# One inversion for all chunks of a delta-rule recurrence, with split masks and units every third step

## The chip, the cores and the metric

The kernel runs on one core of one Trainium2 chip. The metric is the device time of one execution in microseconds (us). Before the change the median of three runs is 2544.13 us (2540.35 to 2546.16).

## What is computed

A two-layer decoder trunk on 272 tokens (16 learned ones and 256 of the input) of width 2048 in float32. Layer 0 mixes tokens with RWKV-7, layer 1 with gated linear attention; an MLP with squared ReLU follows each. The change touches layer 0 alone, whose core in the reference is a step by step recurrence over a 64x64 state for each of 32 heads:

```python
def step(S, inp):
    r_t, w_t, k_t, v_t, a_t, b_t = inp
    sa = jnp.einsum('bhvk,bhk->bhv', S, a_t)
    S = S * w_t[:, :, None, :] + sa[..., None] * b_t[:, :, None, :] + v_t[..., None] * k_t[:, :, None, :]
    y = jnp.einsum('bhvk,bhk->bhv', S, r_t)
    return S, y
```

## The kernel before

The kernel does not step token by token. It cuts the 272 tokens into four chunks of 64 and a short one of 16 (padded to 32). For each chunk and head it forms a score matrix of 128x128 (`AM0` to `AM3`, all 32 heads of a chunk in one tile; `AMr`, 64x64, for the short chunk) whose left half holds what a triangular system needs and whose right half what the output needs. The triangular part of 64x64 is inverted: its two 32x32 diagonal blocks by elimination on VectorE (`eliminate`, 30 steps of two operations), then joined on TensorE (`merge`, a first and a second product with four copies behind each).

Two stages matter here. In the first, the projection of v, TensorE makes 256 steps of three matrix products (`mm3`; a weight tile in two float32r parts, `hi` cast by ScalarE at L132, `lo` subtracted by VectorE at L133, lasts 8 steps). Between the steps the code places score "units": one unit loads four pairs of heads of one chunk (two DMAs into a `ring` of three slots), makes 32 products of scores into two PSUM banks (`scores`, L500; the banks come from the tags `pu` and `pt`, two banks each), and four steps later VectorE multiplies them by a mask into `AM`. There are 16 units of full chunks and 4 of the short one. The chunks 0 and 1 are inverted in this stage (`invert(0)`, from step 49) and merged in it; the chunks 2 and 3 (`invert(1)`) are begun at step 245 and run into the second stage.

The second stage is the recurrence: five chunks, two groups z of 16 heads each, in an order written out by hand. `centre` and `keys` transpose values and keys into place, `inner` and `state` form the right-hand side (two halves of a bank are negated by `sides`, the first by ScalarE, the second by VectorE), `solve` multiplies by the inverse, `learn` updates the state `S`, `emit` makes the output and `gate` the output gate. The merges of chunks 2 and 3 stand in the rounds c = 1 and c = 2 of it.

The order on TensorE and VectorE is the order of the program text (`manual_schedule`). The elimination is cut into pieces, and `fill` puts the next piece into VectorE's order as soon as two clocks of a planner allow it (`pe` and `dve` advance them by costs written in the code; VectorE's may run `slack` us ahead of TensorE's; `fill(True)` empties the queue). ScalarE's and SyncE's orders are left to a scheduler that takes the earliest ready one. Two engines that read one PSUM bank are put one behind the other by semaphores.

Of the kernel before, what the change touches and what calls it, by code (L numbers as in the profile page):

```python
# [17 lines left out]
P = 128  # L18
# [10 lines left out]
C = 64  # L29
# [16 lines left out]
class Kern:  # L46
# [217 lines left out]
    def rwkv(self, done):  # L264
# [222 lines left out]
        TA, X, T2 = (self.t(kp, [P, 32, 32], n) for n in ("TA", "X", "T2"))  # L487
        X4 = T2.rearrange("p a b -> p (a b)")[0:64, :512].rearrange("p (a b) -> p a b", a=16)
        sb = self.t(kp, [P, KT, HEAD], "S")
        amof = lambda c: AMs[c] if c < NC4 else AMr  # L490

        def scores(t, c, g, bank):
# [9 lines left out]
            pe(0.95)  # L502
            return lambda: mask(c, g, pv, n)

        def mask(c, g, pv, n):
            mk = self.maskA if c < NC4 else self.maskR
            for q in range(2):
# [3 lines left out]
        upd = lambda n: self.t(kp, [P, 256], "upd", 1)[:, :n]  # L511
# [24 lines left out]
        def eliminate(X, n, rows):  # L536
            k = rows.stop - rows.start
            x = X[rows]
            for s in range(1, n - 1):
                a, m = n - 1 - s, s  # L540
                yield cost(a * m)
                w = upd(a * m)[rows].rearrange("p (a b) -> p a b", a=a)
                tt(w, x[:, s + 1 : n, s : s + 1].to_broadcast([k, a, m]), x[:, s : s + 1, :m].to_broadcast([k, a, m]))
                yield cost(a * m)
                tt(x[:, s + 1 : n, :m], x[:, s + 1 : n, :m], w, ALU.add)

        def invert(i):
            bands = [(2 * i + a, b) for a in range(2) for b in range(2)]
            diag = lambda c, u: AMs[c][64 + 32 * u : 96 + 32 * u, :, 32 * u : 32 * u + 32]
            halves = (slice(0, 16), slice(16, 32))  # L550
            for b, (c, u) in enumerate(bands):
                nc.scalar.copy(TA[32 * b : 32 * b + 32], diag(c, u))
            for k in halves:
                yield 1.15
                nc.vector.transpose(X[:, k], TA.rearrange("p h t -> p t h")[:, k])
            nc.gpsimd.memset(X.rearrange("p a b -> p (a b)")[:, ::33], 1.0)
            yield from eliminate(X, 32, slice(0, P))
            for k in halves:
# [654 lines left out]
```

## Time and profile before

| | |
|---|---|
| median of 3 runs | 2544.13 us |
| profiled execution | 2551.34 us, its span 2549.6 us |
| TensorE (PE) busy | 98% of the span |
| VectorE (DVE) busy | 64% |
| ScalarE (ACT) busy | 49% |
| granted TensorE clock, mean | 0.994 |
| projection of v | about 282 to 409.7 us |
| recurrence | 409.7 to about 503 us |

A busy TensorE is not one at its peak, since matrix products are pipelined; what tells is where it stands idle and what ended the idle time. An idle VectorE or ScalarE costs nothing by itself.

### The profile page before, as it was taken

How to read it: one execution, taken by the hardware profiler on the slowest of the kernel's cores; microseconds unless marked ns; L12 is line 12 of the kernel's file. 1: busy time of each engine (PE TensorE's matmuls, PEld its weight loads, DVE VectorE, ACT ScalarE, POOL GpSimd, SP SyncE). 2: the span in 40 equal slices, each digit the busy share in tenths (PEclk: the TensorE clock that was granted, in tenths of full speed). 3: DMA queues.
4: the chain of work that ended last, by engine and by line, in shares of the span. 5: the costliest groups of instructions: out<-in, count | busy, mean ns of one | idle time of the engine just before them, and what ended most of it. 6: DMA issues, size and time to landing. Idle time of an engine off the chain costs nothing.

```text
span 2549.6 us, 47710 instructions
## 1 busy us (share of the span) xinstructions
PE 2493.8 (98%) x19636; PEld 2328.4 (91%) x19636; DVE 1638.3 (64%) x2568; ACT 1252.6 (49%) x1990; POOL 7.2 (0%) x31
## 2 busy tenths in 40 slices
PE   7999999899999999999999999999999999999997
PEld 7998898789999999999999999998888888888886
DVE  8777787586555455455456688777666656666565
ACT  5476536464444344344344455544555445445344
POOL 0000000000000000000000000000000000000000
PEclk9999999899999999999999999999999999999999
DMA  5578865155555555555555454445555555555554
GB/s 196 185 244 276 261 213 190 40 177 174 174 174 174 173 169 177 174 173 173 174 173 180 163 168 160 154 156 174 187 187 189 190 187 187 188 190 189 186 189 157
DMA packets 156970, 461.64 MB, mean 181 GB/s; under 512 B 15312, under 2 KB 44240, under 8 KB 156752
## 3 DMA queue, kind: packets, MB, share of 16 engines
q1 hardware_dynamic: 156752, 458.59, 54.6%
q8 instruction: 154, 2.52, 0.4%
q14 instruction: 64, 0.52, 0.1%
HBM read 441.49 MB, written 17.04 MB: 180 GB/s over the span
## 4 chain that ended last, share of the span: by engine, by line
PE 87%; DVE 2%; ACT 2%; DMA 2%; issue 1%; SPq 0%; DVEq 0%; ACTq 0%
PE pj L166 24%; PE pj L138 14%; PE pj L139 14%; PE pj L140 14%; PE pj L167 13%; DMA ca<-cad 1%; DVE lo L133 1%; DMA ard<-ar 1%; PE pt L737 1%; ACT hi L132 0%; PE pu L1051 0%; PE pt L139 0%; PE pt L623 0%; PE pt L140 0%; PE pu L500 0%
## 5 line engine op out<-in xcount | busy, mean ns | idle before, releaser
L132 ACT CAST hi<-raw 128x1024 fp32r<-128x1024 f32 (+2 forms) x820 | 812.8, 997 | 1105.4 <-PE pj L139 586.9
L133 DVE TENSOR_TENSOR lo<-raw,hi 128x1024 fp32r<-128x1024 f32 (+2 forms) x820 | 946.6, 1159 | 613.9 <-ACT hi L132 606.3
L138 PE MATMUL pj<-x,hi 128*128 128x272 f32 x2144 | 624.4, 291 | 4.5 <-ACT x L305 4.5
L139 PE MATMUL pj<-x,hi 128*128 128x272 f32 x2144 | 620.8, 290 | 2.6 <-DVE x L266 2.1
L140 PE MATMUL pj<-x,lo 128*128 128x272 f32 x2144 | 619.3, 289 | 1.0 <-DVE lo L133 0.9
L166 PE MATMUL pj<-x,hi 128*128 128x512 f32 x1664 | 587.3, 396 | 2.1 <-DVE cj L176 1.1
L167 PE MATMUL pj<-x,lo 128*128 128x256 f32 x1664 | 468.5, 282 | 0.8 <-DVE lo L133 0.8
L139 PEld LDWEIGHTS pj<-x,hi 128*128 128x128 f32 x2144 | 407.4, 190 | 5.5 <-DVE x L266 4.6
L138 PEld LDWEIGHTS pj<-x,hi 128*128 128x128 f32 x2144 | 402.9, 188 | 9.2 <-ACT x L305 5.2
L140 PEld LDWEIGHTS pj<-x,lo 128*128 128x128 f32 x2144 | 404.3, 189 | 2.4 <-DVE lo L133 1.8
L166 PEld LDWEIGHTS pj<-x,hi 128*128 128x128 f32 x1664 | 312.9, 188 | 75.0 <-issue 1.9
L166 PE MATMUL pj<-h,hi 128*128 128x512 f32 x1024 | 358.5, 394 | 0.0
L167 PEld LDWEIGHTS pj<-x,lo 128*128 128x128 f32 x1664 | 314.4, 189 | 1.7 <-DVE lo L133 1.1
L138 PE MATMUL pj<-h,hi 128*128 128x272 f32 x1024 | 297.0, 290 | 0.0
L139 PE MATMUL pj<-h,hi 128*128 128x272 f32 x1024 | 295.4, 288 | 0.0
L140 PE MATMUL pj<-h,lo 128*128 128x272 f32 x1024 | 294.7, 288 | 0.0
L167 PE MATMUL pj<-h,lo 128*128 128x256 f32 x1024 | 288.5, 282 | 0.0
L166 PEld LDWEIGHTS pj<-h,hi 128*128 128x128 f32 x1024 | 192.4, 188 | 44.3
L139 PEld LDWEIGHTS pj<-h,hi 128*128 128x128 f32 x1024 | 195.1, 190 | 0.0
L140 PEld LDWEIGHTS pj<-h,lo 128*128 128x128 f32 x1024 | 193.5, 189 | 0.0
L167 PEld LDWEIGHTS pj<-h,lo 128*128 128x128 f32 x1024 | 193.5, 189 | 0.0
L138 PEld LDWEIGHTS pj<-h,hi 128*128 128x128 f32 x1024 | 192.2, 188 | 0.0
(330 smaller groups left out, 2215.7 us busy)
## 6 DMA issues: line engine op xcount, KB each, us to landing
raw<-mlp_w_d SPq DMA_DIRECT2D x512, 512.0 KB, 3.3
raw<-gla_in_d SPq DMA_DIRECT2D x98, 512.0 KB, 3.3
raw<-w_rkv_d SPq DMA_DIRECT2D x80, 512.0 KB, 3.9
raw<-gla_o_d SPq DMA_DIRECT2D x32, 512.0 KB, 3.2
raw<-rw_o_d SPq DMA_DIRECT2D x18, 512.0 KB, 3.3
raw<-w_r_d SPq DMA_DIRECT2D x16, 512.0 KB, 3.4
raw<-rw_oK_d SPq DMA_DIRECT2D x16, 448.0 KB, 3.3
ard<-ar SPq DMA_DIRECT2D x16, 320.0 KB, 4.3
```

The lines of the kernel that those rows point to most:

```text
L132: nc.scalar.copy(hi[:, h], raw[:, h])
L133: nc.vector.tensor_tensor(out=lo[:, h], in0=raw[:, h], in1=hi[:, h].bitcast(F32), op=ALU.subtract)
L138: nc.tensor.matmul(out, hi[:, ws], xh, start=first, stop=False)
L139: nc.tensor.matmul(out, hi[:, ws], xl, start=False, stop=False)
L140: nc.tensor.matmul(out, lo[:, ws], xh, start=False, stop=last)
L166: nc.tensor.matmul(wide, hi[:, ws], x[kt][:, :, off : off + SEQ], start=kt == 0, stop=False)
L167: nc.tensor.matmul(ps[:, :SEQ], lo[:, ws], x[kt][:, 0, off : off + SEQ], start=False, stop=kt == nk - 1)
L737: nc.tensor.matmul(pg, g2s[f // 4][:, f % 4, i], gs[i], start=i == 0, stop=i == 1)
```

## The change

All four chunks are inverted at once: `TA` and `X` hold two layers (the two diagonal blocks) of 128 partitions (four chunks of 32 rows), so that one elimination of 60 operations does twice the elements each. A unit comes every third step from step 4 to step 49, and the elimination starts when the last full unit is masked, at step 55. VectorE masks only the left half of each bank, ScalarE copies the right half unmasked, and `rmask` masks that half later in place, for 16 heads at a time. All eight merge products and the four short units go to the head of the recurrence and to its round c = 0. The load of the next weight tile moves from the second to the third step of a tile, and the gates of round 1 are spread over the rounds 1 and 2.

```diff
+        TA, X = (self.t(kp, [P, 2, 32, 32], n) for n in ("TA", "X"))
         sb = self.t(kp, [P, KT, HEAD], "S")
+        T2 = flat(sb).rearrange("p (a b) -> p a b", a=32)
...
             for q in range(2):
-                dve(0.73 if c < NC4 else 0.44)
-                tt(amof(c)[:, 8 * g + q : 8 * g + 8 : 2], pv[q], mk.unsqueeze(1).to_broadcast([2 * n, 4, 2 * n]))
+                am = amof(c)[:, 8 * g + q : 8 * g + 8 : 2]
+                dve(0.44)
+                tt(am[:, :, :w], pv[q][:, :, :w], mk[:, :w].unsqueeze(1).to_broadcast([2 * n, 4, w]))
+                if w < 2 * n:
+                    nc.scalar.copy(am[:, :, w:], pv[q][:, :, w:])
+
+        def rmask(z, c):
+            if c < NC4:
+                am = AMs[c][:, 16 * z : 16 * z + 16, C:]
+                dve(1.2)
+                tt(am, am, self.maskA[:, C:].unsqueeze(1).to_broadcast([P, 16, C]))
...
+        def gather(c):
+            for u in range(2):
+                at(step + 2 * u, lambda u=u: nc.scalar.copy(TA[band(c), u], diag(c, u)))
+
+        def invert():
+            by_t = lambda u: TA[:, u].rearrange("p h t -> p t h")
+            for u in range(2):
+                for k in halves:
+                    yield 1.15
+                    nc.vector.transpose(X[:, u, k], by_t(u)[:, k])
+            nc.gpsimd.memset(X.rearrange("p u a b -> p u (a b)")[:, :, ::33], 1.0)
+            yield from eliminate(X, 32, flat(sb))
             for k in halves:
                 yield 1.15
+                nc.vector.transpose(T2.rearrange("p h s -> p s h")[:, k], X[:, 0].rearrange("p t s -> p s t")[:, k])
+            for u in range(2):
+                for k in halves:
+                    yield 1.15
+                    nc.vector.transpose(by_t(u)[:, k], X[:, u, k])
+                if u == 0:
+                    nc.scalar.copy(diag(0, 0), TA[band(0), 0])
+                    nc.scalar.copy(t11(0), T2[band(0)])
+                    nc.scalar.copy(diag(1, 0), TA[band(1), 0])
+            for c in range(NC4):
+                yield 0.69
+                nc.vector.tensor_copy(diag(c, 1), TA[band(c), 1])
+                if c in (1, 3):
+                    yield 0.69
+                    nc.vector.tensor_copy(t11(c), T2[band(c)])
+                if c < 2:
+                    nc.scalar.copy(diag(c + 2, 0), TA[band(c + 2), 0])
...
-                    if j == 1 and (f, i) != (KT - 1, 1):
+                    if j == 2 and (f, i) != (KT - 1, 1):
                         ahead()
+                        dve(1.34)
...
-        def unit():
+        def unit(then):
             m = scores(*loaded.pop(0), self.pu if len(order) % 2 else self.ptr)
-            more()
-            return m
+            if order[0][0] < NC4:
+                more()
+            at(step + 4, m)
+            if then:
+                at(step + 4, then)
...
+            then = {6: lambda: gather(0), 7: lambda: gather(1), 11: lambda: gather(2),
+                    15: lambda: (gather(3), at(step + 2, lambda: todo.append([invert(), None])))}
+            for z, c, n in ((0, 0, 28), (1, 0, 31), (0, 1, 34), (1, 1, 37)):
+                at(n, lambda z=z, c=c: rmask(z, c))
+            for k in range(16):
+                at(4 + 3 * k, lambda k=k: unit(then.get(k)))
...
             slack[0] = 0.25
             inner(0, 0)
             sides(0, 0)
             bload(1, 0)
+            more()
             centre(1, 0, ("x", "x"))
             aload(0, 1)
             aload(1, 1)
+            inner(1, 0)
+            sides(1, 0)
+            keys(1, 0)
+            masks = [scores(*loaded.pop(0), self.pu)]
+            more()
+            masks.append(scores(*loaded.pop(0), self.ptr))
+            more()
+            fill(True)
+            for c in range(2):
+                merge(c, (self.pm, self.pry)[c], False, True)
+            masks[0]()
+            for c in range(2):
+                merge(c, (self.pm, self.pry)[c], True, True)
+            masks[1]()
             for c in range(5):
                 if c:
                     state(0, c)
                     learn(1, c - 1)
+                    if c > 1:
+                        rmask(0, c)
                     emit(1, c - 1)
...
                 solve(0, c)
+                if c == 0:
+                    merge(2, self.ptr, False, True)
                 if c < NC4:
                     learn(0, c)
+                    if c > 1:
+                        rmask(1, c)
                 emit(0, c)
+                if c == 0:
+                    merge(3, self.ptr, False, True)
                 solve(1, c)
...
                 if c == 0:
+                    merge(2, self.ptr, True, True)
+                    short(self.ptr)
+                    more()
                     centre(0, 2, ("x", "hi"))
+                    merge(3, self.ptr, True, True)
+                    short(self.ptr)
+                    todo.append([invert_short(), None])
```

`short` makes a unit of the short chunk and masks it at once.

## Rows read from the trace of the kernel before

**Rows 1.** The page, busy time of TensorE, its share of the span, instructions.
```profile
PE 2493.8 (98%) x19636; PEld 2328.4 (91%) x19636; DVE 1638.3 (64%) x2568; ACT 1252.6 (49%) x1990; POOL 7.2 (0%) x31
```

**Rows 2.** Stretches: from:to, length, each engine's busy us, clock, DMA share, GB/s.
```profile
290.00:300.00 10.00, 10.00 (x147) 9.03 (x147) 6.92 (x12) 2.57 (x5) 0.00 (x0) 1.00 0.94 309
...
320.00:351.00 31.00, 31.00 (x271) 30.60 (x269) 28.64 (x69) 12.86 (x25) 0.16 (x1) 1.00 0.54 181
...
392.00:409.70 17.70, 17.70 (x409) 16.49 (x398) 8.36 (x15) 16.24 (x29) 0.00 (x0) 1.00 0.49 162
409.70:423.40 13.70, 12.78 (x309) 11.53 (x308) 12.53 (x33) 10.24 (x21) 0.16 (x1) 1.00 0.56 170
...
443.90:450.40 6.50, 0.00 (x1) 0.00 (x1) 6.26 (x8) 2.08 (x2) 0.00 (x0) 0.85 0.25 81
450.40:455.20 4.80, 4.77 (x72) 3.32 (x72) 1.29 (x3) 0.72 (x2) 0.00 (x0) 0.50 0.02 3
...
464.70:468.90 4.20, 4.20 (x81) 3.80 (x82) 0.68 (x1) 1.76 (x3) 0.00 (x0) 0.59 0.44 126
```

**Rows 3.** TensorE's waits in the recurrence: who, for what, us, times, longest.
```profile
PE pt L583 <- DVE X L568: 6.5, 1, 6.5
PE pry L668 <- issue: 3.2, 1, 3.2
```

**Rows 4.** TensorE in order of time, late projection: a short unit, a merge.
```profile
387.51 0.29 PE L140 MATMUL pj<-x,lo 128*128 128x272 f32 x1
387.73 0.65 PE L500 MATMUL pt<-ring 64*32 64x64 f32 x32
388.31 0.39 PE L138 MATMUL pj<-x,hi 128*128 128x272 f32 x1
...
399.85 0.75 PE L583 MATMUL pm<-X,AM 32*32 32x32 f32 x64
400.53 0.39 PE L138 MATMUL pj<-x,hi 128*128 128x272 f32 x1
```

**Rows 5.** Loads of units (L423): DMA from issue to landing, us.
```profile
DMA to landing us min/median/max: 3.5/4.5/6.9
```

**Rows 6.** VectorE, 320 to 400 us, groups by form: count, busy us, mean ns.
```profile
L133 DVE TENSOR_TENSOR lo<-raw,hi 128x512 fp32r<-128x512 f32 x44 | 28.4, 687 | 9.7 <-ACT hi L132 9.4
L266 DVE TENSOR_TENSOR AM<-pu,cst 128x512 f32<-128x512 f32 x8 | 5.1, 684 | 0.4 <-PE pu L500 0.4
...
L563 DVE STREAM_TRANSPOSE TA<-X 128x512 f32<-128x512 f32 x2 | 2.2, 1100 | 0.0
...
L566 DVE COPY AM<-TA 32x1024 f32<-32x1024 f32 x2 | 1.4, 689 | 0.1
...
L266 DVE TENSOR_TENSOR upd<-X 128x240 f32<-128x240 f32 x2 | 0.8, 408 | 0.1
```

**Rows 7.** ScalarE, 285 to 400 us, groups by form, columns as before.
```profile
L552 ACT COPY TA<-AM 32x1024 f32<-32x1024 f32 x7 | 7.3, 1046 | 4.5 <-DVE AM L266 4.3
L795 ACT COPY hres<-pj 128x272 f32<-128x272 f32 x14 | 5.3, 377 | 0.0
```

**Rows 8.** In order of time: a merge in the recurrence and its copies.
```profile
450.43 1.08 PE L583 MATMUL pt<-X,AM 32*32 32x32 f32 x64 [6.53 <-DVE X L568]
...
451.56 0.36 ACT L593 COPY TA<-pt 32x256 f32<-32x256 f32 x1 [1.29 <-PE pt L583]
451.96 0.42 DVE L591 COPY TA<-pt 32x256 f32<-32x256 f32 x1 [1.68 <-ACT TA L593]
452.41 0.36 ACT L593 COPY TA<-pt 32x256 f32<-32x256 f32 x1 [0.49 <-DVE TA L591]
```

**Rows 9.** The chain of waits: start, us, what (a full unit, solve's copy, centre).
```profile
305.28 1.03 PE pu L500 x32
...
420.13 0.58 ACT x L696
...
421.38 2.05 PE pt L623 x16
```

More of the change, by code (lines that the diff above doesn't have):

```diff
@@ L534, in fill, with eliminate @@
                 todo[0][1] = None
-        def eliminate(X, n, rows):
-            k = rows.stop - rows.start
-            x = X[rows]
+        def eliminate(x, n, scratch):
+            k, b = x.shape[:2]
             for s in range(1, n - 1):
                 a, m = n - 1 - s, s
[L541 to L552, printed above, removed]
+                yield cost(b * a * m)
+                w = scratch[:, : b * a * m].rearrange("p (u a b) -> p u a b", u=b, a=a)
+                tt(w, x[:, :, s + 1 : n, s : s + 1].to_broadcast([k, b, a, m]),
+                   x[:, :, s : s + 1, :m].to_broadcast([k, b, a, m]))
@@ new lines, in eliminate @@
+                yield cost(b * a * m)
+                tt(x[:, :, s + 1 : n, :m], x[:, :, s + 1 : n, :m], w, ALU.add)
+        halves = (slice(0, 16), slice(16, 32))
+        band = lambda c: slice(32 * c, 32 * c + 32)
+        diag = lambda c, u: AMs[c][64 + 32 * u : 96 + 32 * u, :, 32 * u : 32 * u + 32]
+        def gather(c):
[9 more added lines that the diff above has]
+            yield from eliminate(X, 32, flat(sb))
@@ L553, in invert @@
             for k in halves:
                 yield 1.15
[L555 to L558, printed above, removed]
-                yield 1.15
-                nc.vector.transpose(T2.rearrange("p h s -> p s h")[:, k], X.rearrange("p t s -> p s t")[:, k])
-            for k in halves:
-                yield 1.15
-                nc.vector.transpose(TA.rearrange("p h t -> p t h")[:, k], X[:, k])
@@ L795, in v_proj, with short @@
             nc.scalar.copy(hres[:, f], ps)
-        def unit():
+        def unit(then):
             m = scores(*loaded.pop(0), self.pu if len(order) % 2 else self.ptr)
-            more()
-            return m
+            if order[0][0] < NC4:
[3 more added lines that the diff above has]
+                at(step + 4, then)
+        def short(bank):
+            scores(*loaded.pop(0), bank)()
         self.split_parts = 2
@@ L804, in rwkv @@
         with tc.manual_schedule(engines={mybir.EngineType.PE, mybir.EngineType.DVE}):
-            later, step, mstep = [], 0, None
-            at = [16 * f + s for f in range(KT) for s in ((4, 9, 14) if f < 2 else (4, 12) if f == 2 or 8 < f < 15 else ())]
+            step, plan = 0, []
+            at = lambda n, x: plan.append((n, x))
+            clock[:] = [0.0, 3.0]
+            then = {6: lambda: gather(0), 7: lambda: gather(1), 11: lambda: gather(2),
[4 more added lines that the diff above has]
+                at(4 + 3 * k, lambda k=k: unit(then.get(k)))
+            at(249, lambda: (bload(0, 0), centre(0, 0, ("x", "x"))))
+            at(252, lambda: keys(0, 0))
             for f in range(KT):
@@ L810, in rwkv @@
                     pe(0.376)
[L811 to L834 removed]
+                    while due := [x for x in plan if x[0] <= step]:
+                        for x in due:
+                            plan.remove(x)
+                            x[1]()
+                    if step % 16 == 12:
+                        at(16 * f + 21, lambda f=f: (dve(0.44), tt(rr[f], rr[f], hres[:, f])))
+            for x in sorted(plan, key=lambda x: x[0]):
                 x[1]()
[L836 to L837 removed]
             slack[0] = 0.25
```

75 lines of the change are left out of this document (17 added, 58 removed).

## The prediction

> **What bounds the kernel now.** The first view is the page: TensorE is busy 98% of the span [rows 1], so what counts is when it idles, runs at the lower clock, or gets other work. The second is the table of stretches [rows 2]. In the projection of v TensorE is busy 31.00 us of 31.00 while VectorE, in the middle of an elimination, works 28.64: VectorE is nearly full and still hidden. At the projection's end it is ScalarE that is nearly full, 16.24 of 17.70 us, and hidden as well. So in this stage only TensorE's own instructions cost time. In the recurrence it is otherwise: from 443.9 to 450.4 TensorE does nothing, and the list of waits gives the reason [rows 3], the merge of chunk 2 waiting 6.5 us for the end of the second inversion on VectorE. In the stretch behind it the granted clock is 0.50, the level of 1.2 GHz, for 4.8 us [rows 2]. Then comes one wait of 3.2 us that no engine ended [rows 3], inside a run of like products, with a clock of 0.59 behind it [rows 2]. All that the change can remove lies here.
>
> **Part by part.** I write + for time added.
>
> (a) The projection loses four short units and four merge products. By the order of time [rows 4] a short unit takes TensorE from 387.73 to 388.31, 0.58 us, and the products around it start about 0.10 late on either side (0.22 after the last product's start instead of 0.12, and 0.39 instead of 0.29 long): 0.78. A merge takes 399.85 to 400.53, 0.68, and 0.88 with the same edges. 4 x 0.78 + 4 x 0.88 = 6.6: **-6.6**.
>
> (b) Sixteen units now come every third step. A period is three steps (planned at 0.376) and a unit of about 1.22 (its 32 products take 1.03 [rows 9], plus the edges), 2.35 us. It needs 512 KB for the unit and three eighths of a 512 KB weight tile, 0.72 MB, or 307 GB/s. The table of stretches has 309 GB/s at a DMA share of 0.94 where units came every fifth step and three loads had piled up [rows 2], so the queue could carry about 329. That is enough in steady state, with 7% to spare. But a unit's load is issued only when the unit three before it frees its slot, takes 4.5 us at the median and up to 6.9 [rows 5], and the first loads queue behind the last writes of the scores' inputs. I expect the fourth and fifth units to wait about a microsecond each. The last three units all take the `pt` banks, since no load follows them and the length that picks the tag stands still; the second and third of them must wait for the masks of the one before. Bounds: nothing, if loads and masks keep up as they do today, and 7, if each of 13 units waits 0.5. Taken, nearer the low end since no unit waits now: **+3.0**.
>
> (c) The masks. A whole bank costs VectorE 0.684 [rows 6]; half of one I put at 0.42, on the line through 240 elements in 0.408 and 512 in 0.687 (0.16 + 0.00103 per element). 32 halves and eight `rmask` of 1024 elements (1.22 by that line) come to 13.4 + 9.8 = 23.2 instead of 21.9 us, so VectorE gains nothing in total; four of the `rmask` move into the recurrence. ScalarE gets 32 copies of about 0.37 (272 elements take 0.377 [rows 7]), 11.8, and eight gathers of 1.046 instead of four in this stage. Today a copy by ScalarE and one by VectorE out of one bank never overlap: they alternate [rows 8]. So a bank is free after 0.42 + 0.37, hardly later than now, and not after 0.42. The Trainium skill (PSUM — Partial Sum Buffer, section PSUM bank collisions raise a hardware error) says that two engines may not access one bank and quadrant at the same time, reads included, and that the compiler adds a dependency; if the split were read as two engines working side by side, the bank would come free 0.3 us earlier, which nothing in the sum needs. Cost beyond (b): **0**; what hides it is the 31.00 of 31.00, and if that cover went it would be 1.3.
>
> (d) The inversion itself. 60 operations have 19840 elements together. On the line above, with about 0.03 us between two, that is 60 x 0.19 + 20.4 = 31.8 us; ten transposes of 1.10 [rows 6] make 11.0 and six copies of 0.689 make 4.1: 47 us on VectorE, where two inversions of 240 elements take 60 fixed parts, 11 us, more. Steps 57 to 256 with one `centre` and one `keys` give 78 us of TensorE time. 24 pairs of `lo` (planned at 1.34) and 12 products with r (0.44) take 37.5 of them. So 40.5 are free for 47. The planner's own arithmetic agrees: at the last step three transposes and the six copies are left, and after the 6.6 us of TensorE work that stands before `fill(True)` VectorE is still 3.3 us behind. The wait of the second inversion thus does not vanish; it moves to the head of the recurrence.
>
> (e) What leaves the later rounds: the wait of 6.5 [rows 3]; half of the 4.8 us at 0.50, 2.4 [rows 2]; the four merges at 0.7, 2.8. **-11.7**. The wait of 3.2 ended by no engine, with 4.2 x 0.41 = 1.7 behind it, I read as an instruction fetch that came late; such a wait hangs on where fetch and loads fall, and I take half of its 4.9 away: **-2.5** (from 0 to -4.9). The Trainium skill (Runtime: NRT & Kernel Launch, section Instruction fetch mechanics) calls such fetches mostly hidden; the row shows one that is not, and by that rule the sum would be 2.5 lower.
>
> (f) What comes to the head and to round 0: eight merges and four short units on TensorE, 8 x 0.7 + 4 x 0.6: **+8.0**.
>
> (g) The chain at the head. I follow it from the projection's last product. `inner`, the two halves of `sides` one behind the other, `centre` (2.05 [rows 9]) and its copies bring `inner(1, 0)` to about 4 us. Meanwhile VectorE finishes the first layer's transposes at 3.5, and three copies of ScalarE, 1.046 each [rows 7], become ready and stand earlier in the program than `sides(1, 0)`. So ScalarE's half of `sides(1, 0)` comes at about 8, VectorE's waits for it, and behind VectorE's wait are queued the last transpose and all six copies of 0.689. They end at about 14. Then the merges: the four copies of a first product alternate between the engines, 0.36 + 0.05 + 0.42 + 0.05 twice, 1.7 us [rows 8], and VectorE's stand behind the six. Second products and their copies follow: `solve(0, 0)` starts at about 18.5. TensorE's work up to there (two `inner` of 32 products like a full unit's, 1.0 each; `centre` 2.05; `keys` with half as many products, 1.0; two short units; four merges) is 9.1, so it idles about 9; today 0.9 in the whole first round, busy 12.78 of 13.70 [rows 2]. **+9.0**, between 4.5 (if ScalarE takes `sides` before its three copies) and 12.5 (if it takes them even before the copies of `centre`).
>
> (h) Round 0. Two merges, `keys`, `centre`, another merge and two short units all take the two `pt` banks in turn, and each waits for the copies of the one before: 1.7 behind a merge [rows 8], 0.8 for a mask, 1.2 to 2.3 for `centre`. Between `solve(0, 0)` and `learn(0, 0)` only one merge of 0.7 covers the two copies behind `solve`, 0.58 [rows 9] and about 0.69. I count 0.8 + 0.4 + 2.0 + 2.0, about 5: **+5.0** (2 to 7). The load of the last short unit, issued when the one before it is done, takes 4.5 [rows 5] and is hidden under these waits; without them 2 us of it would show. The idle 0.9 of today's first round goes: **-0.9**.
>
> (i) The clock. With TensorE busy half of the time at the head, I expect one stretch at 1.2 GHz, as behind today's 6.5 us of idling [rows 2]: 4.8 x 0.5 = **+2.4**, between 0 and 4.8.
>
> Sum: -6.6 + 3.0 - 11.7 - 2.5 + 8.0 + 9.0 + 5.0 - 0.9 + 2.4 = +5.7. The later rounds lose small waits behind VectorE as well, since its second inversion is gone; I take **-1.5** (0 to -3), and come to **+4.2**. Against the profiled execution, 2551.3 us with a span of 2549.6, that is 2555.5; the profiled execution lies 7.2 above the median of the runs, 2544.1, and the same difference is set against that: **2548**.
>
> **The rivals.** First, slower: the chain of (g) decides. Its place is the stretch between the projection's last product and `state(0, 1)`; its mechanism VectorE standing in order behind ScalarE's half of `sides`, and merges, copies and masks in single file on the banks. If idle time there passes 15 us instead of 14, the change is more than 5.1 us slower, and at the upper bounds of (g), (h) and (i) it is +4.2 + 3.5 + 2.0 + 2.4 = +12, 2556. For it speaks that rows 8 show no overlap between the engines on one bank; against it, that ScalarE's order may favour `sides`. Second, faster: VectorE runs ahead of the planner, whose 1.34 and 1.15 are above the rows, ScalarE takes `sides` first, the units do not wait and the fetch does not come late again: by the lower ends of (b), (g), (h), (i) and (e) that is 3.0 + 4.5 + 3.0 + 2.4 + 2.4 = 15.3 below +4.2, so -11 and 2533; two thirds of it give -6 and 2538. Third, the units: if DMA share reaches 1 and each of 13 units waits 0.5, the projection is no longer bound by TensorE and the change ends 4 higher, 2552. That the change does not do what it says is part of the forecast: the inversion is one, but it is not over when the projection is.
>
> **How the numbers follow.** A measurement of this kernel tells 0.2%, 5.1 us, from no change. Forecast, a move within that, 45%; the chain decides, 25%; the units decide, 10%; faster 20%. So faster 0.20, same 0.45, slower 0.35. The likeliest case's own range is 2539 to 2549. The range of 8 in 10 is 2537 to 2559: its lower end leaves out the last third of the second rival, its upper end is the first rival with 3 of the 4 us of the third on top.
>
> **What would show it.** (a) TensorE's time from the projection's first to its last product about 4 us shorter; longer than before if the units decide. (b) In the first 45 us TensorE waiting on nothing released by an engine before units four and five, and DMA share near 0.95. (d) Three transposes and six copies of VectorE behind the projection. (g) `sides(1, 0)` on VectorE waiting for ScalarE, and `solve(0, 0)` 15 to 20 us after the last product. (e) No wait of 6 us in the later rounds. (i) A clock of 0.5 near the merges. What would make the forecast wrong: `solve(0, 0)` within 13 us of the last product, or idle time of over 20 us up to `state(0, 1)`.

## The result, and the profile after

The changed kernel takes 2557.29 us in the median of its runs, against 2541.28 us of the kernel before beside it: the ratio is 1.005, with a 95% interval of 1.0032 to 1.0068. It is slower, by 8 to 17 us, and the forecast of 2548 us was 9 us too low. One of the nine runs, at a mean clock of 0.75, took 3032 us; the ratio leaves it out and so lies below the quotient of the two medians.

The profiled execution took 2558.32 us, its span 2556.5 us at a mean clock of 0.988. Set against the 2549.6 us of before, that is only 7 us more, and the two spans can't be compared as wholes: in the MLP behind the recurrence, whose code is the same, the products follow one another every 124.8 ns in this execution and every 126.7 ns in the profiled execution of before, some 11 us over that stage, and this differs from execution to execution (last section). So I compare stretches. From the first unit's product to the end of `emit(1, 4)` the kernel before takes 218.1 us (285.1 to 503.2) and the changed one 235.7 us (286.7 to 522.4): **17.6 us more**.

The page has TensorE at the same 98% as in [rows 1]:

```profile
PE 2493.0 (98%) x19636; PEld 2327.0 (91%) x19636; DVE 1632.2 (64%) x2522; ACT 1260.6 (49%) x2015; POOL 7.1 (0%) x30
```

That share hides the loss, since a product at half speed counts as busy. The stretches of the changed kernel, with the columns of [rows 2]: the projection from its first unit on, the head up to `solve(0, 0)` in two parts, round 0 in two, and what follows.

```profile
286.70:413.00 126.30, 120.20 (x1293) 113.94 (x1292) 97.35 (x182) 62.12 (x124) 0.22 (x1) 0.99 0.62 202
413.00:421.00 8.00, 5.23 (x86) 4.55 (x86) 3.08 (x4) 6.53 (x10) 0.00 (x0) 0.90 0.59 194
421.00:433.00 12.00, 7.47 (x324) 6.36 (x324) 8.73 (x15) 5.43 (x10) 0.00 (x0) 0.50 0.44 134
433.00:446.70 13.70, 13.28 (x381) 11.83 (x382) 5.78 (x12) 5.38 (x12) 0.00 (x0) 0.50 0.02 4
446.70:457.50 10.80, 6.66 (x180) 5.79 (x168) 2.45 (x7) 3.85 (x9) 0.00 (x0) 0.81 0.35 99
...
470.00:522.40 52.40, 50.32 (x1244) 43.81 (x1233) 29.58 (x53) 24.91 (x51) 1.58 (x2) 0.96 0.20 61
```

Before, TensorE had next to no idle time in the projection [rows 2]; here it is busy 120.2 of 126.3 us. Before, the whole way from the projection to `state(0, 1)` took 13.7 us at full clock, 12.78 of it busy; here it takes 44.5 us, and from 419.3 to 446.7 the granted clock is 0.50, the level of 1.2 GHz. In the fourth row TensorE is busy 13.28 of 13.70 us and the clock stays there all the same: what is slow is not idle time alone. In the last row the 6.5 us of idling of [rows 3] are gone.

TensorE's waits, columns as in [rows 3]: first those in the projection, then those from the projection's end to `state(0, 1)`.

```profile
PE pt L502 <- ACT AM L515: 3.0, 2, 2.1
PE pt L502 <- DMA ring<-ard: 2.8, 2, 1.6
...
PE pt L502 <- DVE AM L618: 3.1, 2, 1.6
PE pt L662 <- ACT x L655: 2.4, 1, 2.4
PE pry L610 <- issue: 2.3, 2, 1.2
PE pm L610 <- DVE X L618: 1.4, 1, 1.4
```

Of the first row, 2.1 us end with the landing of a load, issued at 317.11 and landed at 323.20 just before the product at 323.33, though a copy of ScalarE is named; so 4.9 of the 5.8 us lie behind loads. Below, short units wait for banks that merge copies still read (3.1), `keys(1, 0)` waits for a copy of `centre` (2.4), and 2.3 us were ended by no engine (`issue` in the row). In all profiles of this case the waits of this last kind in the recurrence end 2.2 to 3.4 us behind the start of a 16 KB fetch of instructions, most of them 2.2 to 2.5, so I take them for waits for instructions.

Why `keys` waits shows in ScalarE's and VectorE's order of time at the head:

```profile
417.14 1.04 ACT L582 COPY AM<-TA 32x1024 f32<-32x1024 f32 x1
418.09 1.04 ACT L583 COPY X<-S 32x1024 f32<-32x1024 f32 x1
419.14 1.04 ACT L584 COPY AM<-TA 32x1024 f32<-32x1024 f32 x1
420.20 0.58 ACT L655 COPY x<-pt 64x512 f32<-64x512 f32 x1
420.80 0.59 ACT L669 ACTIVATE x<-pj 64x512 f32<-64x512 f32 x1
...
421.43 0.69 DVE L671 TENSOR_SCALAR x<-pj 64x512 f32<-64x512 f32 x1 [3.90 <-ACT x L669]
422.13 1.06 DVE L580 STREAM_TRANSPOSE TA<-X 128x512 f32<-128x512 f32 x1
```

ScalarE takes the inversion's three copies ahead of the last copy of `centre` and of its half of `sides(1, 0)` (L669). VectorE waits 3.90 us for that half, with the last transpose and the six copies queued behind.

### The profile page after: what moved, and what is told of

It is laid out like the page before. It is cut to its first block, busy times and chain, and to the rows that moved or that the text cites. A ratio compares the mean times of both kernels' runs of the same rounds, so it can differ in the third digit from the quotient of the medians.

```text
span 2556.5 us, 47690 instructions
## 1 busy us (share of the span) xinstructions
PE 2493.0 (98%) x19636; PEld 2327.0 (91%) x19636; DVE 1632.2 (64%) x2522; ACT 1260.6 (49%) x2015; POOL 7.1 (0%) x30
## 4 chain that ended last, share of the span: by engine, by line
PE 91%; DVE 3%; DMA 3%; ACT 2%; issue 1%; SPq 0%; DVEq 0%; ACTq 0%
PE pj L166 24%; PE pj L138 15%; PE pj L139 15%; PE pj L140 15%; PE pj L167 12%; DVE lo L133 1%; PE pj L193 1%; DMA ca<-cad 1%; ACT hi L132 1%; PE pt L139 1%; DMA ard<-ar 1%; PE pt L140 1%; PE pt L138 1%; PE pt L764 0%; PE pt L650 0%
```

## The experiments

Each kernel is the changed one with the edit shown, except where it says otherwise. "Units" is the time from the first unit's product to the first product of `inner(0, 0)`, which follows the projection's last one directly; "solve" and "state" count from there to `solve(0, 0)` and `state(0, 1)`; "low" is the time at 1.2 GHz from the projection's end to `state(0, 1)`; "all" runs from the first unit to the end of `emit(1, 4)`. All in us, each from one profiled execution; the ratio to the kernel before has its 95% interval. The line numbers in the rows shift by some lines from edit to edit.

| kernel | units | solve | state | low | all | ratio |
|---|---|---|---|---|---|---|
| before | 124.6 | 3.4 | 13.6 | 0 | 218.1 | |
| changed | 126.3 | 20.0 | 44.5 | 31.4 | 235.7 | 1.005 (1.0032 to 1.0068) |
| copies late | 123.9 | 18.5 | 43.0 | 24.8 | 233.4 | 1.0025 (1.0006 to 1.0044) |
| 3 products more | 123.0 | 20.6 | 45.1 | 24.5 | 232.7 | 1.0033 (1.0016 to 1.005) |
| 13 products more | 124.3 | 19.6 | 42.2 | 17.0 | 230.4 | 1.003 (1.0012 to 1.0048) |
| every fourth step | 120.6 | 18.5 | 42.6 | 25.0 | 226.0 | 1.0021 (1.0001 to 1.0041) |
| urgent copies | 123.8 | 19.6 | 43.4 | 24.8 | 233.3 | 1.007 (1.0043 to 1.0097) |
| urgent, fourth step | 121.6 | 17.9 | 42.0 | 24.5 | 229.9 | 1.0035 (1.001 to 1.006) |
| whole masks | 123.0 | 20.1 | 42.3 | 21.7 | 229.6 | 1.0043 (1.0021 to 1.0066) |
| GpSimd helps | 143.2 | 15.6 | 38.4 | 18.0 | 244.7 | 1.0117 (1.0077 to 1.0158) |
| urgent, later loads | 122.9 | 15.3 | 37.3 | 18.1 | 225.3 | 1.0037 (1.0013 to 1.006) |
| all together | 121.0 | 15.5 | 35.3 | 20.5 | 226.6 | 1.0026 (1.0004 to 1.0049) |
| dense merges | 124.0 | 18.7 | 41.2 | 20.5 | 229.5 | 1.009 (1.0061 to 1.0119) |

The ratios carry the difference in the MLP with them and are uncertain by 0.2 to 0.4%; "all" is the better measure of an edit. It has a scatter of its own, though: in the seven kernels whose edits leave the units alone, the changed one among them, "units" still runs from 122.9 to 126.3, so a difference of 3 us between two single profiles shows nothing by itself.

### Units every fourth step

```diff
-            for z, c, n in ((0, 0, 28), (1, 0, 31), (0, 1, 34), (1, 1, 37)):
+            for z, c, n in ((0, 0, 37), (1, 0, 41), (0, 1, 45), (1, 1, 49)):
...
-                at(4 + 3 * k, lambda k=k: unit(then.get(k)))
+                at(4 + 4 * k, lambda k=k: unit(then.get(k)))
```

> Edit: the sixteen units come every fourth step instead of every third (and rmask with them); the inversion's start thereby moves 15 steps back. Theory (loads set the units' waits): the waits of 1.17, 1.63 and 2.08 us behind loads go; from the first unit's product to the projection's last product 119 to 121 us instead of 126.3; the inversion, begun some 6 us later, ends 3 to 5 us later at the head, so that last product to solve(0,0) is 23 to 25 instead of 20.0; the kernel 1 to 4 us faster than the changed one. Rival (split masks and ScalarE's copies are what the units wait for): waits of the same sum stay, released by ScalarE or VectorE, and the projection still takes 125 or more.

The projection took 120.6 us. TensorE's waits in it, from 280 to 345 us:

```profile
PE pu L502 <- DMA ring<-ard: 1.1, 2, 0.6
PE pt L502 <- DMA ring<-ard: 0.8, 1, 0.8
```

1.9 us behind loads instead of 4.9, and none behind a bank. That is the theory, and "all" is 9.7 us less than in the changed kernel, where 1 to 4 were expected. On the head it was wrong, in a telling way: the inversion, begun later, was further behind, but `solve(0, 0)` came at 18.5, not at 23 to 25. The first layer's transposes ended so late that ScalarE's half of `sides(1, 0)` (410.14) stood ahead of the three copies (from 412.56), and VectorE waited 0.87 us for it, not 3.90.

### Whole masks by VectorE

```diff
-            w = n if c < NC4 else 2 * n
+            w = 2 * n
...
-            if c < NC4:
+            if False:
                 am = AMs[c][:, 16 * z : 16 * z + 16, C:]
```

> Edit: VectorE masks each whole score bank as in the kernel before; no copies of the other half by ScalarE, no rmask. Prediction's own point (c), the split masks cost nothing and save nothing: from the first unit's product to the projection's last product 126 to 127 us as in the changed kernel (126.3), the same waits behind loads, state(0,1) 43 to 46 after the last product, the kernel within 2 us of the changed one. Rival (ScalarE's 32 copies hold the banks or the loads): the waits behind loads and banks shrink by 3 us or more. Rival (the split frees VectorE, so that the inversion is earlier): solve(0,0) 2 us or more later than 20.0.

The units took 123.0 us, with 4.2 us of waits behind three loads; the other kernels with units every third step have 122.9 to 126.3. `solve(0, 0)` came at 20.1. Within this spread the split masks thus cost and save nothing, as (c) has it; the expected 126 to 127 was the changed kernel's own profile, which lies at the upper end of its kind. Two more expectations failed: `state(0, 1)` came at 42.3, not at 43 to 46, and "all" is 6.1 us less than in the changed kernel, not within 2, 3.3 of it in the projection.

### The three copies behind all transposes

```diff
-                if u == 0:
-                    nc.scalar.copy(diag(0, 0), TA[band(0), 0])
-                    nc.scalar.copy(t11(0), T2[band(0)])
-                    nc.scalar.copy(diag(1, 0), TA[band(1), 0])
+            nc.scalar.copy(diag(0, 0), TA[band(0), 0])
+            nc.scalar.copy(t11(0), T2[band(0)])
+            nc.scalar.copy(diag(1, 0), TA[band(1), 0])
```

> Edit: the three ScalarE copies (diag(0,0), t11(0), diag(1,0)) stand behind the second layer's transposes instead of between the layers. Theory (single file at the head, and a low clock that has its own cause): VectorE's wait of 3.90 us ahead of its half of sides(1,0) falls to under 1.5, TensorE's wait of 2.40 ahead of keys(1,0) falls to under 1; from the projection's last product to solve(0,0) 17 us instead of 20.0, to state(0,1) about 41.5 instead of 44.5; the granted clock is still 0.5 for over 20 us; the kernel about 3 us faster than the changed one. Rival (that wait of 2.40 us is what brings the clock down): the clock stays at 1.0 up to state(0,1), which comes at about 31 us after the last product; the kernel 12 to 14 us faster than the changed one, so level with the kernel before or 3 us behind it.

The wait ahead of `keys` went, and VectorE waited 1.8 us instead of 3.9. But `solve(0, 0)` came only 1.5 us earlier, at 18.5. TensorE's idle time up to it did not shrink, 7.4 us against 7.3: the waits for instructions grew from 2.35 to 3.27 us, and other waits for copies came. What was gained are products at full clock, since the clock fell later:

```profile
411.00:422.40 11.40, 8.39 (x277) 7.13 (x276) 8.13 (x11) 9.95 (x14) 0.00 (x0) 1.00 0.80 244
422.40:442.90 20.50, 15.67 (x492) 13.88 (x496) 9.47 (x21) 7.15 (x18) 0.00 (x0) 0.50 0.06 20
```

It begins 11.4 us behind the projection instead of 6.3 and lasts 20.5 us, without the wait that the rival made its cause. The rival fell; of the theory's price of 3, half came, and not by the way that it named.

### Only the urgent copies first, and the loads behind them

```diff
...
+            nc.scalar.copy(t11(0), T2[band(0)])
+            nc.scalar.copy(diag(0, 1), TA[band(0), 1])
+            yield 0.69
+            nc.vector.tensor_copy(t11(1), T2[band(1)])
+            yield 0.69
+            nc.vector.tensor_copy(diag(1, 1), TA[band(1), 1])
...
-                merge(c, (self.pm, self.pry)[c], False, True)
+                merge(c, (self.pm, self.pry)[c], False, 2 * c)
...
+                    rest()
```

The last argument of `merge` tells who copies: 0 is ScalarE alone, 2 VectorE alone. `rest` makes the other copies, behind `solve(0, 0)`.

> Edit: at the head only the copies that the first two merges need stand before them (t11(0) and diag(0,1) on ScalarE, t11(1) and diag(1,1) on VectorE), ScalarE makes all copies of chunk 0's merges and VectorE all of chunk 1's, diag(0,0) follows between the merges, and the other six copies follow solve(0,0). Same products, same copies. Theory (the single file of copies sets the head): solve(0,0) at 13 to 15 us after the projection's last product instead of 20.0, state(0,1) at 37 to 39 instead of 44.5, the clock still 0.5 for some 15 to 20 us; the kernel 5 to 7 us faster than the changed one. Rival (the merges' products and the late instructions of 1.1 to 1.2 us set the head, the copies are hidden behind them): solve(0,0) at 18 or later.

The waits from the projection's end to `state(0, 1)`:

```profile
PE pry L613 <- issue: 4.0, 1, 4.0
PE pt L502 <- DVE AM L621: 3.1, 2, 1.6
PE pu L722 <- DVE AMr L266: 2.3, 1, 2.3
```

The theory failed: `solve(0, 0)` came at 19.6, in the rival's range. The copies were out of the way, and the first merges followed the short units without a gap; then TensorE stood 4.02 us in the middle of the second merge, ended by no engine. The trace has a fetch of instructions of 16 KB at 416.8 and the next at 424.7, with 433 of TensorE's instructions (weight loads counted) between the two, and four loads under way from 419.2 to 427.8. The 2.3 us are my own edit's: I had put the first short unit's mask behind the second merges, and it held the `pu` bank that `solve` needs. With units every fourth step the same edit gave:

> Edit: the copies of the edit before, and units every fourth step. Theory (the two losses stand one behind the other and add up): from the first unit's product to the projection's last product 119 to 121 us as with every fourth step alone (120.6), solve(0,0) 13.5 to 15 us after it instead of 18.5, state(0,1) 36 to 38 instead of 42.6; the kernel 4 to 5 us faster than with every fourth step alone, about level with the kernel before. Rival (the inversion, begun 15 steps later, is what the head waits for): solve(0,0) stays at 17 to 18.5.

121.6, 17.9 and 42.0: the units add up but for 0.6 us, the head does not. 17.9 is in the rival's range, though the inversion is only part of it: the first merges wait 1.8 us for its copies, and the same 2.3 us and 2.4 us of waits without a releaser lie ahead of `state(0, 1)`. The next kernel puts the mask back and lets ScalarE issue two of the loads at their place in its order:

```diff
-            nc.sync.dma_start(BKz[z], bkd[c][:, 8 * z : 8 * z + 8])
+            (nc.scalar if c == 1 else nc.sync).dma_start(BKz[z], bkd[c][:, 8 * z : 8 * z + 8])
```

> Edit: as with only the urgent copies ahead of the first merges, with the first short unit's mask back between first and second merges (behind them it held solve(0,0) for 2.35 us), and the two loads bload(0,1) and bload(1,1), 512 KB each, issued by ScalarE at their place in its order, behind the merges' copies, instead of by SyncE as soon as a slot is free. Theory (loads in flight delay the fetch of TensorE's instructions: 433 instructions passed between two fetches, then 4.02 us of waiting while four loads were under way): the wait without a releaser falls from 4.02 to under 1.3 in all up to solve(0,0), which comes 13.5 to 15.5 us after the last product instead of 19.6. Rival (the fetch is late by itself when 32x32 products follow one another closely): 2.5 us or more of such waits stay before solve(0,0), which comes at 16 or later.

```profile
PE pt L502 <- DVE AM L621: 3.1, 2, 1.6
PE pry L613 <- issue: 2.0, 2, 1.3
PE pry L613 <- DVE X L621: 1.0, 1, 1.0
```

`solve(0, 0)` came at 15.3 and `state(0, 1)` at 37.3. The waits without a releaser up to `solve(0, 0)` fell from 4.0 to 2.0 us, between the two expectations. That fits loads in flight as a part of their cause, but does not show it: kernels that leave these loads alone have anything from 0.9 (whole masks) to 4.0 us of such waits. The Trainium skill (Runtime: NRT & Kernel Launch, section Instruction fetch mechanics) calls a fetch mostly hidden. At the merges of the head the trace disagrees in all changed kernels that keep the 32 products of a merge, with 0.5 to 4.0 us of such waits up to `solve(0, 0)`.

### GpSimd makes half of `lo`

```diff
-                nc.vector.tensor_tensor(out=lo[:, h], in0=raw[:, h], in1=hi[:, h].bitcast(F32), op=ALU.subtract)
+                eng = nc.gpsimd if i == 1 and getattr(self, "lo_pool", False) else nc.vector
+                eng.tensor_tensor(out=lo[:, h], in0=raw[:, h], in1=hi[:, h].bitcast(F32), op=ALU.subtract)
...
+                        self.lo_pool = 57 <= step < 248
...
-                        dve(1.34)
+                        dve(0.67 if self.lo_pool else 1.34)
```

> Edit: from step 57 to 247 of the projection GpSimd, idle until now, makes the second half of every `lo`; VectorE keeps the first. Nothing else moves. It takes 24 x 0.69 = 16.5 us from VectorE while it inverts. Theory (VectorE's load in the projection is why the inversion reaches into the head, and the copies there are what the head waits for): the inversion and its copies are over 6 to 10 us before the projection's last product; no wait for the copies of t11 and diag is left at the head; solve(0,0) 11.5 to 13.5 us after the last product instead of 20.0, state(0,1) at 33 to 38 instead of 44.5; the kernel 7 to 11 us faster than the changed one. Rival (merges and late instructions set the head): solve(0,0) at 16 or later though no copy is waited for. Rival (GpSimd is too slow, or slows VectorE beside it): TensorE waits for `lo` in the projection, which becomes longer than 126.3 from the first unit on.

The planner counts half for such a `lo`. GpSimd's group, and VectorE's from 345 to 395 us, where it inverts; columns as in [rows 6]. Behind them the same two operations in the changed kernel, the products with r as shortest, median and longest in ns:

```profile
L134 POOL TENSOR_TENSOR lo<-raw,hi 128x512 fp32r<-128x512 f32 x24 | 34.3, 1427 | 220.9 <-ACT hi L132 207.4 <-DVE S L267 5.9 <-DVE lo L134 4.7
```

```profile
L267 DVE TENSOR_TENSOR r<-r,hres 128x272 f32<-128x272 f32 x7 | 6.3, 900 | 0.0
...
L267 DVE TENSOR_TENSOR X<-X,S 128x480 f32<-128x480 f32 x2 | 2.4, 1200 | 0.0
```

```profile
L266 DVE TENSOR_TENSOR r<-r,hres x12: 427/433/441, 346.3 to 413.6; 128x272 f32<-128x272 f32 x12
```

```profile
L266 DVE TENSOR_TENSOR X<-X,S 128x480 f32<-128x480 f32 x2 | 1.3, 659 | 0.1
```

GpSimd takes 1427 ns where VectorE takes 687. VectorE's products of 272 elements go from 433 to 900 ns in the mean, those of 480 into `X` from 659 to 1200; the two of 480 into `S`, which met no operation of GpSimd, stay at 654. In order of time, one operation on each:

```profile
360.37 1.43 POOL L134 TENSOR_TENSOR lo<-raw,hi 128x512 fp32r<-128x512 f32 x1 [1.88 <-ACT hi L132]
...
360.70 1.58 DVE L267 TENSOR_TENSOR S<-X 128x440 f32<-128x440 f32 x1
362.32 0.62 DVE L267 TENSOR_TENSOR X<-X,S 128x440 f32<-128x440 f32 x1
```

An operation of 440 elements that takes 0.61 us alone takes 1.58, and ends 0.48 us after GpSimd's. That agrees with the Trainium skill (SBUF — State Buffer, section SBUF: two separate sides), by which a VectorE operation with two inputs in SBUF and a GpSimd operation that reads it exclude each other for a whole instruction. TensorE's waits, first in the projection, then up to `state(0, 1)`:

```profile
PE pj L141 <- DVE lo L134: 11.4, 15, 3.0
```

```profile
PE pry L611 <- issue: 3.7, 2, 3.1
```

TensorE waited 11.4 us for `lo`, and the second rival holds. The head of this kernel still answers a question: all copies of the inversion were done, TensorE waited for none of them, and `solve(0, 0)` came at 15.6, with 3.7 us of waits without a releaser. So a head without these copies is 4.4 us shorter than the 20.0, not the 6.5 to 8.5 that I expected, and only 2.1 of that is idle time; the rest are products at full clock, since the clock fell later, 10.2 us behind the projection.

### What the clock hangs on

Three products that nobody reads, in the wait ahead of `keys`; then thirteen, at every larger wait:

```diff
+        def warm(n, bank):
+            ps = bank()[:, :T]
+            for _ in range(n):
+                nc.tensor.matmul(ps, self.bones, rr[0], start=True, stop=True)
...
             sides(1, 0)
+            warm(3, self.pj)
             keys(1, 0)
```

> Edit: three products that nobody reads (bones x rr[0], 272 columns, 0.78 us each by the rows of L432) between sides(1,0) and keys(1,0), where TensorE waits 2.40 us; nothing else moves. Rival (that one wait brings the clock down): with TensorE busy there the clock stays at 1.0, and state(0,1) comes at about 34 us after the last product instead of 44.5. Theory (the clock's loss hangs on how the whole head is filled, not on one wait): the clock still goes to 0.5 within the merges, at most a few us later; state(0,1) at 42 to 45.

> Edit: thirteen such products, three ahead of keys(1,0), one ahead of the first merges, three ahead of the second merges, and three ahead of each short unit of round 0; nothing else moves. Theory (the clock follows how TensorE is filled in this stretch): the clock is at 1.0 for all or most of it; of the 10.2 us that the clock costs in the changed kernel some 8 come back, of 13 x 0.78 = 10.2 us of added products about 8 lie in waits, so state(0,1) at 36 to 40 us after the last product instead of 44.5, and the kernel 5 to 8 us faster than the changed one. If the clock did not hang on TensorE's work, the products would take 1.57 each at 0.5, about 20 us together, of which half lie in waits, and state(0,1) would come at 50 or later.

With three:

```profile
425.10:445.60 20.50, 15.94 (x506) 14.14 (x510) 9.37 (x21) 6.76 (x16) 0.00 (x0) 0.50 0.07 25
```

The clock was at 0.5 from 425.1 for 20.5 us and `state(0, 1)` came at 45.1. The rival fell again. With thirteen:

```profile
410.80:426.20 15.40, 11.80 (x293) 9.57 (x293) 9.45 (x14) 11.17 (x17) 0.00 (x0) 1.00 0.64 204
426.20:443.20 17.00, 15.69 (x459) 13.50 (x458) 8.16 (x18) 5.54 (x13) 0.00 (x0) 0.50 0.02 5
443.20:453.00 9.80, 8.52 (x222) 6.55 (x220) 2.44 (x6) 4.41 (x10) 0.00 (x0) 1.00 0.38 110
```

From 443 on the clock stayed up where the short units' waits had been, and 17.0 us were low instead of 31.4. The direction is the theory's, but `state(0, 1)` came at 42.2, 2 us behind its range: a stretch of 17 us remained, in which TensorE was busy 15.69.

The last of these makes each merge nearly one product of full size:

```diff
-            for h in range(32):
-                o, k = 32 * (h % 4), 32 * (h // 4)
+            for h in range(4):
...
+            nc.tensor.matmul(pq[:, :256], self.bones, rr[0][:, :256], start=True, stop=True)
```

> The changed kernel with, in all eight merges, 4 of the 32 products of 32x32 left in place (so that every wait stays) and the other 28 replaced by one product of 128x128 by 256 columns; the merged blocks, and with them the output, are then other values. Same copies, same waits for copies; the added product takes about 0.74 us by the 0.78 of 272 columns, a merge's 32 take 0.68 to 0.75 at full clock. Theory (the clock falls at small products in a stretch half idle, and the late instructions come with them): the granted clock stays at 1.0 for most of the head and round 0, the two waits without a releaser (1.13, 1.21) go, and state(0,1) comes 31 to 35 us after the last product instead of 44.5. Rival (idle time alone, some 9 us of waits behind copies that stay, brings the clock down): 0.5 for 17 us or more again, state(0,1) at 40 to 43.

```profile
410.60:418.60 8.00, 5.24 (x87) 4.58 (x87) 3.08 (x4) 6.56 (x10) 0.00 (x0) 1.00 0.58 194
418.60:422.00 3.40, 3.40 (x77) 2.76 (x76) 2.94 (x4) 3.33 (x5) 0.00 (x0) 0.50 0.47 86
422.00:425.40 3.40, 1.28 (x12) 0.45 (x10) 3.28 (x6) 0.91 (x3) 0.00 (x0) 1.00 0.96 322
425.40:435.70 10.30, 8.79 (x129) 6.15 (x131) 6.09 (x15) 3.47 (x9) 0.00 (x0) 0.50 0.05 21
435.70:442.50 6.80, 5.30 (x131) 3.81 (x128) 2.90 (x6) 3.78 (x8) 0.00 (x0) 1.00 0.15 42
442.50:449.30 6.80, 6.14 (x54) 5.04 (x54) 0.93 (x3) 2.32 (x4) 0.00 (x0) 0.50 0.39 115
```

The waits without a releaser are gone, as the theory said; the clock's part of it fell. 20.5 us were low and `state(0, 1)` came at 41.2, in the rival's range. Each fall lies in or just behind a wait: of 2.39 us up to 418.40, of 2.65 up to 426.49, of 1.62 up to 442.83. So the clock falls also without 28 of the 32 small products of each merge; it needs neither a full set of them nor waits for instructions. What ends a low stretch (after 3.4 us here, after 20.5 in six kernels) is not shown by these runs and stays open.

### All that helped, together

Every fourth step, the urgent copies, the later loads, `keys(1, 0)` between the merges, the second short unit's mask ahead of them, and in round 0 other banks, of which the cut shows a part:

```diff
-                    merge(3, self.ptr, False, True)
+                    merge(3, self.pry, False, True)
...
-                    short(self.ptr)
+                    short(self.pu)
```

> Edit, all that the runs so far point to: units every fourth step; the urgent copies first, with chunk 0's merge copies on ScalarE and chunk 1's on VectorE; bload(0,1) and bload(1,1) issued by ScalarE at their place; keys(1,0) between first and second merges, where it covers the wait for their copies; in round 0 the merges of chunk 3 in `pry` and the short units in `pu`, so that they don't queue for the two `pt` banks. Theory (the prices add up): from the first unit's product to the projection's last product 120 to 121 us; solve(0,0) 14 to 16 us after it instead of 20.0; from there to state(0,1) 18 to 20 instead of 24.5, with waits under 2 in place of 4.1; state(0,1) 32.5 to 35.5 after the last product instead of 44.5; in all 15 to 18 us less than the changed kernel up to state(0,1), which is level with the kernel before, ratio 0.998 to 1.002. Rival (the clock, 0.5 for 14 to 20 us in every variant, eats the rest): solve(0,0) to state(0,1) stays at 22 or more, ratio 1.002 to 1.004.

Up to `state(0, 1)` the prices nearly added up: 121.0, 15.5, 19.8 from `solve` to `state` and 35.3 are in their ranges, with 2.7 us of waits in the 19.8 instead of under 2, and 14.6 us less in all than in the changed kernel instead of 15 to 18. But "all" is 226.6, 8.5 us above the kernel before, and the ratio is 1.0026, so it is not level with it. From `state(0, 1)` on it takes 70.3 us, 5.4 more than the changed kernel, and the largest of TensorE's waits there is:

```profile
PE pj L694 <- issue: 3.4, 1, 3.4
```

A wait without a releaser of 3.4 us came in round 1, with 6.8 us at 0.5 from just before its end: the pair that [rows 3] and [rows 2] show in the kernel before, and that the changed kernel had been free of. Even without those 5.4 us this kernel would stand 3 us above the one before. No version here beats the kernel before.

### The kernel before once more

> The kernel before, unchanged, profiled a second time. Its executions lie near 2540 or near 2552 us, seldom between. In its first profile (2551.3) the products of the first layer's second half, from 675 to 1440 us, follow one another every 126.7 ns; in all profiles of changed kernels so far every 124.8 ns, 11.4 us less over that stretch, with the same code there. Theory (that stretch alone makes the two groups, and it belongs to the execution, not to the change): a profile near 2552 shows 126.7 ns again, one near 2540 shows 124.8, and the recurrence is the same to 1 us in both. Rival (the change itself quickens that stretch): 126.7 ns whatever the time.

The profile took 2553.67 us and had 126.7 ns again; its recurrence repeats the first profile within 0.2 us (13.5 to `state(0, 1)`, 80.0 from there to the end of `emit(1, 4)`, with the waits of 6.5 and 3.2 us in the same places). That fits the theory and refutes nothing: an execution near 2540 did not come under the profiler. The rival, that the change quickens the stretch, fell by other rows: four changed kernels (dense merges, later loads, both with urgent copies) had 126.7 ns as well.

## Why the prediction was right or wrong

The ratio lies above no change, where the prediction gave 0.35; its likeliest case, a move within 5.1 us at 0.45, did not come. The time lies inside the range, near its upper end, where the first rival put it (2556), and that is in part luck: the range's end allows 15 us more than the 2544.1 that the forecast stands on, the stretches show 17.6, and the kernel before beside it happened to measure 2541.28. The rival's place and VectorE's wait behind `sides` are as it says, but not its condition: idle time up to `state(0, 1)` was 11.9 us and did not pass 15. In the prediction's order:

- **(a)** Right. With units every fourth step TensorE's busy time from the first unit on is 118.5 us against 124.4 before: -5.9 instead of -6.6.
- **(b)** The kind was right, the size was not. Waits behind loads of 1.17, 1.63 and 2.08 us, at the fourth, eighth and fourteenth units, and one of 0.96 behind a bank at the sixteenth, where the last units share the `pt` banks. With a low clock of 3.4 us behind them, the projection is 7.8 longer than its 118.5 of work; 3.0 was taken and 7 was the bound. The sign of (a) turned by it: from the first unit on the projection is 1.7 longer than before, not 4 shorter. The step that failed is "nearer the low end since no unit waits now": from 290 to 310 us the queue moved 284 GB/s at a share of 0.88, where 307 were wanted and 329 thought possible, so the queue was not full; the units' loads of 256 KB landed 3.6 to 6.5 us after issue. The other kernels with every third step lose 4.4 to 5.8.
- **(c)** Right within the spread of the profiles: 0 (whole masks).
- **(d)** Right to the instruction: behind the projection come three transposes and six copies of VectorE.
- **(e)** Right. From `state(0, 1)` to the end of `emit(1, 4)` it is 64.9 us instead of 79.9: -15.0, where -11.7, -2.5 and -1.5 were counted. The late fetch that I half took away did go, with 1.5 us of shorter waits for instructions in its place; the other kernels have 0.6 to 4.0 us of them there, "all together" the most, so that half of it was a fair price and its going here in part luck.
- **(g), (h)** The mechanism was right, with VectorE standing 3.90 us behind ScalarE's `sides`, and so was the idle time: 7.3 us up to `solve(0, 0)` (9.0 expected) and 4.6 in round 0 (5.0). Of the 7.3, 2.35 were waits for instructions, which (g) did not have. That was the error of my first experiments too: with the copies out of the way, the fetch took their place.
- **(i)** This is the term that was mis-sized. From the projection's end to `state(0, 1)` there are 30.9 us more than before (44.5 - 13.6). The work moved there is 8.0 by (f), idle time grew by 10.9 (11.9 - 0.9, rounded); what remains, 12.0, is products that run at half speed (TensorE is busy for 25 of the 31.4 us at 0.5, half of which is 12.5), against 2.4 in the sum and 4.8 as its upper end. The prediction took the one stretch behind the one wait of 6.5 us as its measure. Here the clock fell within the wait of 2.40 us and stayed down for 27.3 us, 13.7 of them with TensorE busy for 97%.

With (b) 4.8 and (i) 9.6 higher, (a) and (e) 0.7 higher each and the idle time 2.2 lower, the sum of +4.2 becomes +17.8; measured are 17.6.

## What to carry to other kernels

Small, dependent steps are cheap where dense work stands around them in an engine's order and dear where they stand alone: a merge product costs 0.88 us in the projection before [rows 4] and, at the head, its own time, its waits, the fetch of its instructions and the clock on top. When work leaves a covered stage, price a good part of the stretch that receives it at the lower clock level (here 17 to 31 of 35 to 45 us, in every version), and look for the rows in which the clock stays low while the engine is busy. Removing one wait in a chain shows only the next one: here copies, a mask and the instruction fetch took turns.

## What the runs showed of the hardware

- A clock of 0.5 lasted 13.7 us with TensorE busy 13.28 of them. In the kernel before, every stretch at 0.5 in the recurrence was over in 6.8 us.
- TensorE waited up to 4.02 us for instructions in a run of 32x32 products, 433 instructions, weight loads counted, after the fetch before. With 28 of a merge's 32 products replaced by one (dense merges), no such wait was left up to `state(0, 1)`.
- A GpSimd operation on 128x512 elements held back the VectorE operations with two inputs that met it: products of 272 elements went from 433 to 900 ns in the mean.
- The same products at the same granted clock of 1.00 run at two speeds, in different executions. The MLP of the first layer from 900 to 1100 us, in the changed kernel and in the one before profiled again, columns as in [rows 2]:

```profile
900.00:1100.00 200.00, 200.00 (x1604) 200.00 (x1603) 102.29 (x116) 81.91 (x99) 0.00 (x0) 1.00 0.53 177
```

```profile
900.00:1100.00 200.00, 200.00 (x1581) 200.00 (x1580) 101.18 (x115) 80.56 (x99) 0.00 (x0) 1.00 0.52 174
```

1604 products in 200 us against 1581, with no idle time in either. The cause is open. Over the whole stage it makes about 11 us, more than the change itself is measured to cost by the ratio's lower bound, and whoever compares two profiles of this kernel by their spans measures this.
